# First attention: score tiles of 32 queries of four heads, over 288 key columns

## The chip, the cores and the metric

The kernel runs on one core of a Trainium2 chip. The core has four compute engines with queues of their own: TensorE (PE, matrix products into the PSUM banks; PEld is its weight load), VectorE (DVE), ScalarE (ACT) and GpSimd (POOL). SyncE (SP) computes nothing and issues most of the transfers. Sixteen DMA engines move data between the chip's DRAM and the on-chip SBUF. The metric is the device time of one execution in microseconds, lower is better.

## The reference

One layer of an encoder, batch 1, 2048 tokens, width 1024, all in float32. The input is normalised, one product with `w_in` gives the queries, keys and values of two attentions and two gates, each attention's result is projected and gated, the two are added, go through `w_out` and onto the input, and a two-layer MLP (1024 to 4096 to 1024, squared ReLU) and a last normalisation follow.

The change lies in the first attention. It has 8 query heads of width 64 and 2 key/value heads, four query heads to each. A token sees the tokens at a distance of at most 128; a slope per head times the distance is taken from the score, and a learned sink logit per head takes part in the softmax:

```
q_pos = i * A_BLOCK + jnp.arange(A_BLOCK)
k_pos = (i - 1) * A_BLOCK + jnp.arange(3 * A_BLOCK)
dist = jnp.abs(q_pos[:, None] - k_pos[None, :])
valid = (dist <= A_WINDOW) & (k_pos[None, :] >= 0) & (k_pos[None, :] < s)
sc = jnp.einsum('bqkgd,bskd->bkgqs', qi, ki).astype(jnp.float32) * scale
sc = sc - slopes[:, :, None, None] * dist.astype(jnp.float32)
sc = jnp.where(valid, sc, -jnp.inf)
...
p = jax.nn.softmax(jnp.concatenate([sc, sink_col], axis=-1), axis=-1)[..., :-1]
...
```

The probabilities `p` are then multiplied with the values. With blocks of 128 queries, a block touches 384 keys, though a single query sees only 257 of them.

## The kernel before, in words

Every float32 operand of a product is split in two parts, a high one rounded to a narrower format (fp32r) and the low rest. ACT makes the high part with a copy, DVE or POOL the low part with a subtraction, and a product takes two or three matmuls. All matmuls take 128 rows of weights and up to 512 columns.

The stages, in order of time:

1. Input projection (`in_quad`, 0 to about 360 us). Blocks of 512 tokens are called b; b = 0 and 1 are projected here with a scheme of seven products for eight (the products are numbered by `ORDER`, results fall due at numbers 2, 7, 4 and 3). PE's banks are emptied by DVE additions (the helper at L290) and ACT copies (L498). A result of the q and k features goes through `qk_parts` (L426): ACT writes the high part (L443 for the first attention, with the scale; L439 for the second), DVE the low part (L444, L440), both into one buffer `ze` of a ring of two, and SP stores it to DRAM (L464). A buffer may be filled again when its store has landed. On the same ACT queue stand the casts of the next weights (`zwhl`, L293), on the same DVE queue their low parts (L294) and the emptying of the banks.
2. First attention (L747 `attn_a`, about 360 to 660 us). A unit is one key/value head g and one block i of 128 queries: 32 units. For each of the four heads h, two matmuls (L764, L765) give scores of 128 queries by 384 keys (256 for the first and last block). The stored q has 64 rows of high and 64 of low parts, the keys are loaded in two arrangements, so two matmuls give all four part products. DVE adds the bias (a tile of distances times the head's slope, made by POOL at L731), takes the row's maximum together with the sink and writes to the SBUF tile `sa` (L766). ACT takes the exponential and the row sums (L773), a few operations of four columns handle the sink (L769 to L775), POOL multiplies by the reciprocal (L777). PE turns the probabilities, 128 by 128 at a time, into the bank `pt` (L784), ACT and DVE split them (L787, L788), and PE multiplies them with the values (L789, L790) into a bank `av`. ACT and DVE add its two halves into `ya` (L793, L794), which SP stores to `y_a`.
3. Between the units, `paced` puts dense filler: the projection of blocks b = 2 and 3 by plain three-matmul products (`mm`, L200 to L202). Its q results go through the same `qk_parts` into a ring of three buffers `z` and are stored at L705 (417 to 488 us).
4. Second attention (to about 1030 us, also with dense filler), gates and output projection, then the two MLP products to the end.

The order of the instructions on each engine is not written out by hand: the program order above is reordered by the framework's planner, which simulates the program with its own costs while it builds it. `issue_after` holds single instructions behind others.

In DRAM, q of the first attention is `qs_a[g][m]`, laid out `[128, 4, 8, 128]`: row of parts, head, block, query (m is the half of the tokens). A store of one result tile (128 features, so two heads, by 512 tokens) is two DMAs of 128 runs of 512 floats. The load of a unit (L757) takes 4 runs of 128 floats from each of 128 rows.

Of the kernel before, what the change touches and what calls it, by code (L numbers as in the profile page):

```python
# [8 lines left out]
F32 = mybir.dt.float32  # L9
F32R = mybir.dt.float32r  # L10
AF = mybir.ActivationFunctionType
ALU = mybir.AluOpType
# [10 lines left out]
P = 128  # L23
KC = D // P
NB = 4
BT = 512
ROWS = 32
GW = 64
NEG = -1.0e30


O_QA, O_KA, O_VA, O_QB, O_KB, O_VB, O_GA, O_GB = 0, 512, 640, 768, 1280, 1792, 2304, 3328
# [30 lines left out]
def host_constants():  # L63
    import numpy as np

    q = np.arange(128)[:, None]
    k = np.arange(384)[None, :] - 128
# [25 lines left out]
def encoder_layer(ctx, tc, x, norm_mix, w_in, b_gate, sink, rpb, w_pa, w_pb, w_out,  # L93
                  norm_mlp, w_up, w_down, norm_final, dist_a, mask_b, out):
    nc = tc.nc
    V, A, G, PE, SY = nc.vector, nc.scalar, nc.gpsimd, nc.tensor, nc.sync
# [16 lines left out]
    dp = pool("dp", space=DRAM)  # L113
# [20 lines left out]
    sink_t = cp.tile([P, AH], F32, name="sink_t")  # L134
# [13 lines left out]

    qs_a = [[dp.tile([P, 4, 8, P], F32, name=f"qs_a{g}{m}") for m in range(2)] for g in range(2)]
    ks_a = [dp.tile([2, P, S // 2], F32, name=f"ks_a{m}") for m in range(2)]
    vs_a = [dp.tile([2, P, 8, P], F32, name=f"vs_a{m}") for m in range(2)]
    qs_b = [dp.tile([2, P, 4, 4, P], F32, name=f"qs_b{t}") for t in range(4)]
# [271 lines left out]
    def qk_parts(col, b, src, t2):  # L426

        th, tl = t2[:, 0], t2[:, 1]
        if O_QB <= col < O_VB:
            if col < O_KB:  # L430

                pv = src.rearrange("p (r j c) -> p j r c", r=8, j=4)
                hv, hr, lr = (flipped(t) for t in (th, th.bitcast(F32R), tl.bitcast(F32R)))
            else:

                pv = src.rearrange("p (q r x) -> p q r x", q=2, r=4)
                hv, hr, lr = (t.rearrange("p (q x r) -> p q r x", q=2, r=4)
                              for t in (th, th.bitcast(F32R), tl.bitcast(F32R)))
            A.copy(hr, pv)  # L439
            V.tensor_tensor(out=lr, in0=pv, in1=hv, op=ALU.subtract)  # L440
        else:
            scale = 1.0 if col == O_KA else 0.125
            A.activation(th.bitcast(F32R), src, AF.Copy, scale=scale)  # L443
            last_low[0] = V.scalar_tensor_tensor(out=tl.bitcast(F32R), in0=src, scalar=scale, in1=th,  # L444
                                                 op0=ALU.mult, op1=ALU.subtract).ins
        parts = [(e, t2[e * 64 : e * 64 + 64]) for e in range(2)]
        if col < O_KA:
            dst, h = qs_a[col // 256][b // 2], col // P % 2 * 2
            dst = dst.rearrange("(z p) h i q -> p z h (i q)", z=2)
            return [(dst[:, :, h + e, b % 2 * BT : (b % 2 + 1) * BT], t) for e, t in parts]  # L450
        if O_QB <= col < O_KB:
            dst = qs_b[(col - O_QB) // P]
            return [(dst[e].rearrange("(z p) b j q -> p z b (j q)", z=2)[:, :, b], t) for e, t in parts]
        dst, o = (ks_a[b // 2], b % 2 * BT) if col == O_KA else (ks_b[(col - O_KB) // P], b * BT)
        return [(dst[e].rearrange("(z p) t -> p z t", z=2)[:, :, o : o + BT], t) for e, t in parts]
# [215 lines left out]
    ap_ = pools(s_a, "left", ("ka1", "va1", "qa", "sta", "sa", "ya", "dist", "ph", "pl", "biasa1"), "a")  # L671
    ap_.update(pools(s_a, "right", ("biasa0", "va0", "ka0"), "a"))
    hp = {}

# [46 lines left out]
            yield  # L721


    dist = T(ap_, [P, 384], F32, "dist", 1)
    SY.dma_start(dist, dist_a)
    bias_a = [None] * 2

    def make_bias_a(g):
        t = T(ap_, [P, 4, 384], F32, f"biasa{g}", 1)
        for h in range(4):  # L730
            G.tensor_scalar(t[:, h], dist, 2.0 ** -(4 * g + h + 1), 1.0, ALU.mult, ALU.mult)  # L731
        bias_a[g] = t

    done, began, shares = [], [], []

    kas = [T(ap_, [P, 2, S], F32R, f"ka{g}", 1) for g in range(2)]
    vas = [T(ap_, [P, 16, P], F32R, f"va{g}", 1) for g in range(2)]

    def load_kv(g, m, behind=None):
        k, kd = kas[g][:, :, m * (S // 2) : (m + 1) * (S // 2)], ks_a[m][g]  # L740
# [5 lines left out]

    def attn_a(g, i):  # L747
        c0, c1 = (1 if i == 0 else 0), (2 if i == 15 else 3)
        lo, hi = c0 * P, c1 * P
        n = hi - lo  # L750
        if bias_a[g] is None:

            with tc.issue_after(shares[2]):
                make_bias_a(g)
        base = (i - 1) * P
        q = T(ap_, [P, 4, P], F32R, "qa", 3)
        began.append(SY.dma_start(q.bitcast(F32), qs_a[g][i // 8][:, :, i % 8]).ins)  # L757
        ka, v = kas[g], vas[g]
        s = T(ap_, [P, 4, 384], F32, "sa", 4)
        st = T(ap_, [P, 8, 4], F32, "sta", 8)  # L760
        mx, nm, sm, es, ri = (st[:, k, :] for k in range(5))
        for h in range(4):
            ps = psum("s", 3)
            PE.matmul(ps[:, :n], q[:, h, :], ka[:, 0, base + lo : base + hi], start=True, stop=False)  # L764
            PE.matmul(ps[:, :n], q[:, h, :], ka[:, 1, base + lo : base + hi], start=False, stop=True)  # L765
            V.tensor_tensor_reduce(out=s[:, h, lo:hi], in0=ps[:, :n], in1=bias_a[g][:, h, lo:hi], scale=1.0,  # L766
                                   scalar=sink_t[:, 4 * g + h : 4 * g + h + 1], op0=ALU.add, op1=ALU.max,
                                   accum_out=mx[:, h : h + 1])
        A.activation(nm, mx, AF.Copy, scale=-1.0)  # L769
        V.tensor_tensor(out=es, in0=sink_t[:, 4 * g : 4 * g + 4], in1=mx, op=ALU.subtract)  # L770
        A.activation(es, es, AF.Exp)
        for h in range(4):
            A.activation(s[:, h, lo:hi], s[:, h, lo:hi], AF.Exp, bias=nm[:, h : h + 1], accum_out=sm[:, h : h + 1])  # L773
        V.tensor_tensor(out=sm, in0=sm, in1=es, op=ALU.add)
        V.reciprocal(ri, sm)  # L775
        for h in range(4):
            share = G.tensor_scalar(s[:, h, lo:hi], s[:, h, lo:hi], ri[:, h : h + 1], 1.0, ALU.mult, ALU.mult)  # L777
        shares.append(share.ins)
        yield
        po = psum("av", 1)  # L780
        for c in range(c0, c1):
            pt = psum("pt", 2)
            for h in range(4):
                PE.transpose(pt[:, h * P : (h + 1) * P], s[:, h, c * P : (c + 1) * P], ident)  # L784
            ph = T(ap_, [P, 512], F32R, "ph", 3)
            pl = T(ap_, [P, 512], F32R, "pl", 3)
            A.copy(ph, pt)  # L787
            V.tensor_tensor(out=pl, in0=pt, in1=ph.bitcast(F32), op=ALU.subtract)  # L788
            PE.matmul(po, v[:, i - 1 + c, :], ph, start=c == c0, stop=False)  # L789
            last = PE.matmul(po, v[:, i - 1 + c, :], pl, start=False, stop=c == c1 - 1).ins  # L790
        done.append(last)
        t = T(ap_, [64, 512], F32, "ya", 2)
        A.copy(t, po[64:128, :])  # L793
        V.tensor_tensor(out=t, in0=po[0:64, :], in1=t, op=ALU.add)  # L794
# [841 lines left out]
```

## Time and profile before

| | |
|---|---|
| median of three executions | 2621.41 us (2618.64, 2621.41, 2622.58) |
| span of the profiled execution, first to last instruction | 2620.1 us |
| mean granted TensorE clock | 0.999 |
| PE busy | 2586.9 us, 99% |
| DVE, ACT, POOL busy | 62%, 47%, 14% |
| DMA | 490.30 MB, 353982 packets, 28792 of them under 512 B |

The profile holds one execution. Engine lines give busy time; rows of groups read: line, engine, operation, output <- inputs, shape, count, then busy time and mean duration, then the idle time of the engine ahead of them and what ended it. Rows of windows read: stretch, its length, busy time of PE, PEld, DVE, ACT, POOL, then the granted clock, the share of the DMA engines' time and GB/s. Rows of waits read: who waited for whom, total, times, longest. Matmuls are pipelined: the recorded duration of one is longer than the distance to the next.

### The profile page before, as it was taken

To read this page: it belongs to the slowest core of one execution; us is meant where nothing else is said; L and a number is where in the kernel's file an instruction comes from. 1 tells how busy PE (TensorE), PEld (TensorE's weight loads), DVE (VectorE), ACT (ScalarE), POOL (GpSimd) and SP (SyncE) were. 2 spreads that over 40 slices of the span, in tenths; PEclk is the share of its full clock that TensorE was granted. 3 is DMA by queue.
4 is the path that set the end of the run, shared out by engine and by line. 5 is a ranking of instruction groups with operands and counts; after the bars stand their busy time and mean duration, and the time that the engine had idled before them with its cause. 6 is when DMAs were issued, how large, how long until landed. Compare 5 with 4: busy or idle time off the path is not lost.

```text
span 2620.1 us, 34509 instructions
## 1 busy us (share of the span) xinstructions
PE 2586.9 (99%) x12140; PEld 2149.8 (82%) x12140; DVE 1625.1 (62%) x2653; ACT 1239.8 (47%) x2261; POOL 358.1 (14%) x431
## 2 busy tenths in 40 slices
PE   8999999999999999999999999999999999999999
PEld 6888788778888888888888888888888888888887
DVE  8765666665544444755567777776656534555766
ACT  5335256666555555633334554644544322322454
POOL 1000114344555541000001000100000000000010
PEclk9999999999999999999999999999999999999999
DMA  5657485455876655954556655854428825445555
GB/s 184 200 156 200 141 243 159 114 155 145 240 219 180 191 144 164 318 177 151 179 178 208 245 205 202 302 191 149 153 101 300 300 101 182 146 146 171 183 194 170
DMA packets 353982, 490.30 MB, mean 187 GB/s; under 512 B 28792, under 2 KB 188664, under 8 KB 351632
## 3 DMA queue, kind: packets, MB, share of 16 engines
q1 hardware_dynamic: 346752, 471.04, 56.8%
q10 hardware_dynamic: 7056, 17.04, 1.8%
q8 instruction: 96, 1.57, 0.2%
q14 instruction: 78, 0.64, 0.1%
HBM read 328.54 MB, written 159.45 MB: 186 GB/s over the span
## 4 chain that ended last, share of the span: by engine, by line
PE 88%; DVE 4%; DMA 4%; ACT 2%; issue 1%; SPq 1%; POOL 0%; DVEq 0%; POOLq 0%; ACTq 0%
PE b L297 15%; PE b L299 15%; PE b L298 15%; PE mm L200 6%; PE mm L202 6%; PE mm L201 6%; PE zb L297 3%; PE zb L299 3%; PE zb L298 2%; PE pt L200 2%; PE pt L201 2%; PE pt L202 2%; PE av L967 2%; PE pt L955 2%; PE s L927 2%
## 5 line engine op out<-in xcount | busy, mean ns | idle before, releaser
L298 PE MATMUL b<-dwh,dah 128*128 128x512 f32 x896 | 348.5, 389 | 0.0
L299 PE MATMUL b<-dwh,dah 128*128 128x512 f32 x896 | 347.6, 389 | 0.0
L297 PE MATMUL b<-dwh,dah 128*128 128x512 f32 x896 | 339.6, 389 | 0.0
L293 ACT CAST dah<-da 128x1024 fp32r<-128x1024 f32 (+1 forms) x128 | 120.9, 945 | 368.6 <-PE b L299 241.8
L294 DVE TENSOR_TENSOR dah<-da,dah 128x1024 fp32r<-128x1024 f32 (+1 forms) x128 | 139.7, 1091 | 224.1 <-ACT dah L293 221.1
L297 PE MATMUL b<-ubh,uwhlb 128*128 128x512 f32 x592 | 230.3, 389 | 0.0
L298 PE MATMUL b<-ubh,uwhlb 128*128 128x512 f32 x592 | 230.3, 389 | 0.0
L299 PE MATMUL b<-ubh,uwhlb 128*128 128x512 f32 x592 | 229.3, 389 | 0.1
L200 PE MATMUL mm<-hT,whl 128*128 128x512 f32 x544 | 218.2, 401 | 0.0
L202 PE MATMUL mm<-hT,whl 128*128 128x512 f32 x544 | 215.1, 395 | 0.0
L201 PE MATMUL mm<-hT,whl 128*128 128x512 f32 x544 | 213.7, 393 | 0.0
L298 PEld LDWEIGHTS b<-dwh,dah 128*128 128x128 f32 x896 | 168.2, 188 | 35.0
L299 PEld LDWEIGHTS b<-dwh,dah 128*128 128x128 f32 x896 | 168.2, 188 | 34.9
L297 PEld LDWEIGHTS b<-dwh,dah 128*128 128x128 f32 x896 | 168.2, 188 | 34.9
L297 PE MATMUL zb<-zh,zwhl 128*128 128x512 f32 x476 | 186.7, 394 | 7.9 <-DVE zc L290 3.4
L298 PE MATMUL zb<-zh,zwhl 128*128 128x512 f32 x476 | 186.4, 392 | 0.0
L299 PE MATMUL zb<-zh,zwhl 128*128 128x512 f32 x476 | 183.7, 392 | 0.3 <-DVE zwhl L294 0.3
L290 DVE TENSOR_TENSOR uc<-b,uc 128x512 f32<-128x512 f32 x160 | 109.2, 689 | 104.2 <-PE b L299 103.2
L1506 POOL TENSOR_TENSOR st<-st,power 128x1 f32<-128x1 f32 x16 | 13.3, 841 | 925.0 <-DVE st L1505 924.9
L297 PEld LDWEIGHTS b<-ubh,uwhlb 128*128 128x128 f32 x592 | 111.1, 188 | 23.8 <-issue 0.4
L299 PEld LDWEIGHTS b<-ubh,uwhlb 128*128 128x128 f32 x592 | 111.1, 188 | 23.5 <-DVE uwhlb L294 0.5
L298 PEld LDWEIGHTS b<-ubh,uwhlb 128*128 128x128 f32 x592 | 111.1, 188 | 23.1
(253 smaller groups left out, 5912.5 us busy)
## 6 DMA issues: line engine op xcount, KB each, us to landing
at<-uc SPq DMA_DIRECT2D x224, 256.0 KB, 2.0
da<-at SPq DMA_DIRECT2D x96, 512.0 KB, 3.7
dw<-in_w_down_dram SPq DMA_DIRECT2D x160, 256.0 KB, 4.8
uraw<-in_w_up_dram SPq DMA_DIRECT2D x32, 1024.0 KB, 6.8
raw<-in_w_in_dram SPq DMA_DIRECT2D x34, 512.0 KB, 4.7
zraw<-in_w_in_dram SPq DMA_DIRECT2D x16, 1024.0 KB, 7.7
z<-zg SPq DMA_DIRECT2D x64, 256.0 KB, 5.1
qa<-qs_a SPq DMA_DIRECT2D x32, 256.0 KB, 8.3
```

The source lines that it names most:

```text
L200: PE.matmul(ps, lh, rh, start=first, stop=False)
L201: PE.matmul(ps, lh, rl, start=False, stop=False)
L202: PE.matmul(ps, ll, rh, start=False, stop=last)
L290: return eng.tensor_tensor(out=out, in0=a, in1=b, op=op).ins
L293: A.copy(hi, src)
L294: return eng.tensor_tensor(out=lo, in0=src, in1=hi.bitcast(F32), op=ALU.subtract).ins
L297: PE.matmul(ps, lh, rh, start=first, stop=False, skip_group_check=True)
L298: PE.matmul(ps, lh, rl, start=False, stop=False, skip_group_check=True)
L299: PE.matmul(ps, ll, rh, start=False, stop=last, skip_group_check=True)
L927: PE.matmul(ps[:, :n], q[:, i, :], kv[:, z, B_R0[i] // 4 : (B_R0[i] + B_NR[i]) // 4, 4 * B_C0[j] : 4 * (B_C0[j] + w)], start=z == 0, stop= ...
L955: PE.transpose(pt[:kp, at + (i - i0) * P : at + (i - i0 + 1) * P], s[i][:, rr : rr + kp], ident)
L967: last = PE.matmul(po[:, i0 * P : (i0 + ni) * P], v[:kp, c, :], src[:kp, o : o + ni * P], start=first, stop=(c == 7 and z == 1), skip_grou ...
```

## The change

A score tile still has 128 rows, but they are 32 consecutive queries of all four heads of the group, instead of 128 queries of one head. The 32 queries see 288 keys, so a tile is 288 columns wide instead of 384; a unit again has four tiles, u = 0 to 3, each 32 keys further on. What follows from it:

- The bias is one tile of 288 columns for each group, the distance times a slope that now differs by row; slopes and sinks are laid out by row (`by_head`, POOL).
- The probabilities of tile u stand in columns 32u to 32u + 288 of 384. The transposes take all 384, so the columns outside must be zero: the four `sa` buffers are allocated once, POOL clears those columns once (24 memsets), and the units take the buffers in turn.
- The sink's part is one ACT exponential with a bias by row, instead of a DVE subtraction and an ACT exponential.
- The columns of `av` are ordered by tile, head and query; the last copy and addition read it by head.
- q is laid out in DRAM as `[128, 32, 4, 32]`: row, group of 32 queries, head, query. A load takes one run of 512 floats from each row. A store writes runs of 32 floats, and is four DMAs of 1024 runs instead of two of 128.

```
-    qs_a = [[dp.tile([P, 4, 8, P], F32, name=f"qs_a{g}{m}") for m in range(2)] for g in range(2)]
+    qs_a = [[dp.tile([P, 32, 4, A_Q], F32, name=f"qs_a{g}{m}") for m in range(2)] for g in range(2)]
...
-            dst = dst.rearrange("(z p) h i q -> p z h (i q)", z=2)
-            return [(dst[:, :, h + e, b % 2 * BT : (b % 2 + 1) * BT], t) for e, t in parts]
+            n = BT // A_Q
+            dst = dst.rearrange("(z p) u h q -> p z u h q", z=2)[:, :, b % 2 * n : (b % 2 + 1) * n]
+            return [(dst[:, z, :, h + e], t[:, z].rearrange("p (u q) -> p u q", u=n)) for e, t in parts for z in range(2)]
...
-    dist = T(ap_, [P, 384], F32, "dist", 1)
+    dist = T(ap_, [P, A_K], F32, "dist", 1)
...
+    by_head = T(ap_, [P, 4], F32, "byhead", 1)
+    slope, sink_p = by_head[:, 0:2], by_head[:, 2:4]
+    for h in range(4):
+        at = slice(h * A_Q, (h + 1) * A_Q)
+        for g in range(2):
+            G.memset(slope[at, g : g + 1], 2.0 ** -(4 * g + h + 1))
+        G.tensor_copy(out=sink_p[at], in_=sink_t[at].rearrange("p (g h) -> p g h", g=2)[:, :, h])
...
-        t = T(ap_, [P, 4, 384], F32, f"biasa{g}", 1)
-        for h in range(4):
-            G.tensor_scalar(t[:, h], dist, 2.0 ** -(4 * g + h + 1), 1.0, ALU.mult, ALU.mult)
+        t = T(ap_, [P, A_K], F32, f"biasa{g}", 1)
+        G.tensor_scalar(t, dist, slope[:, g : g + 1], 1.0, ALU.mult, ALU.mult)
...
+    sas = [T(ap_, [P, 4, 384], F32, "sa", 4) for _ in range(4)]
+    for t in sas:
+        for u in range(4):
+            for lo, hi in ((0, u * A_Q), (u * A_Q + A_K, 384)):
+                if lo < hi:
+                    G.memset(t[:, u, lo:hi], 0.0)
...
-        q = T(ap_, [P, 4, P], F32R, "qa", 3)
-        began.append(SY.dma_start(q.bitcast(F32), qs_a[g][i // 8][:, :, i % 8]).ins)
+        q = T(ap_, [P, 4, 4, A_Q], F32R, "qa", 3)
+        s = sas[len(began) % 4]
+        began.append(SY.dma_start(q.bitcast(F32), qs_a[g][i // 8][:, i % 8 * 4 : i % 8 * 4 + 4]).ins)
...
-        for h in range(4):
+        span = [(max(u * A_Q, c0 * P), min(u * A_Q + A_K, c1 * P)) for u in range(4)]
+        for u, (lo, hi) in enumerate(span):
+            n = hi - lo
             ps = psum("s", 3)
-            PE.matmul(ps[:, :n], q[:, h, :], ka[:, 0, base + lo : base + hi], start=True, stop=False)
-            PE.matmul(ps[:, :n], q[:, h, :], ka[:, 1, base + lo : base + hi], start=False, stop=True)
+            for z in range(2):
+                PE.matmul(ps[:, :n], q[:, u].rearrange("p h q -> p (h q)"), ka[:, z, base + lo : base + hi],
+                          start=z == 0, stop=z == 1)
...
-        V.tensor_tensor(out=es, in0=sink_t[:, 4 * g : 4 * g + 4], in1=mx, op=ALU.subtract)
-        A.activation(es, es, AF.Exp)
+        A.activation(es, mx, AF.Exp, bias=sink_g, scale=-1.0)
...
-        A.copy(t, po[64:128, :])
-        V.tensor_tensor(out=t, in0=po[0:64, :], in1=t, op=ALU.add)
+        t4 = t.rearrange("d (h u q) -> d h u q", h=4, u=4)
+        by_u = po.rearrange("p (u h q) -> p h u q", u=4, h=4)
+        A.copy(t4, by_u[64:128])
+        V.tensor_tensor(out=t4, in0=by_u[0:64], in1=t4, op=ALU.add)
```

The DVE bias addition, the exponential and the normalisation go over the same 288 columns in the same way.

More of the change, by code (lines that the diff above doesn't have):

```diff
@@ L29 @@
 NEG = -1.0e30
+A_Q = 32
+A_K = A_Q + 256
 O_QA, O_KA, O_VA, O_QB, O_KB, O_VB, O_GA, O_GB = 0, 512, 640, 768, 1280, 1792, 2304, 3328
@@ L64, in host_constants @@
     import numpy as np
-    q = np.arange(128)[:, None]
-    k = np.arange(384)[None, :] - 128
+    q = np.arange(128)[:, None] % A_Q
+    k = np.arange(A_K)[None, :] - 128
     dist = np.abs(q - k)
@@ L670, in encoder_layer @@
     s_a = ExitStack()
-    ap_ = pools(s_a, "left", ("ka1", "va1", "qa", "sta", "sa", "ya", "dist", "ph", "pl", "biasa1"), "a")
+    ap_ = pools(s_a, "left", ("ka1", "va1", "qa", "sta", "sa", "ya", "dist", "ph", "pl", "biasa1", "byhead"), "a")
     ap_.update(pools(s_a, "right", ("biasa0", "va0", "ka0"), "a"))
@@ L748, in attn_a @@
         c0, c1 = (1 if i == 0 else 0), (2 if i == 15 else 3)
-        lo, hi = c0 * P, c1 * P
-        n = hi - lo
         if bias_a[g] is None:
@@ L755, in attn_a @@
         base = (i - 1) * P
-        q = T(ap_, [P, 4, P], F32R, "qa", 3)
-        began.append(SY.dma_start(q.bitcast(F32), qs_a[g][i // 8][:, :, i % 8]).ins)
+        q = T(ap_, [P, 4, 4, A_Q], F32R, "qa", 3)
+        s = sas[len(began) % 4]
+        began.append(SY.dma_start(q.bitcast(F32), qs_a[g][i // 8][:, i % 8 * 4 : i % 8 * 4 + 4]).ins)
         ka, v = kas[g], vas[g]
-        s = T(ap_, [P, 4, 384], F32, "sa", 4)
         st = T(ap_, [P, 8, 4], F32, "sta", 8)
         mx, nm, sm, es, ri = (st[:, k, :] for k in range(5))
-        for h in range(4):
+        sink_g = sink_p[:, g : g + 1]
@@ L763, in attn_a @@
+        span = [(max(u * A_Q, c0 * P), min(u * A_Q + A_K, c1 * P)) for u in range(4)]
+        for u, (lo, hi) in enumerate(span):
+            n = hi - lo
             ps = psum("s", 3)
[L764 to L768, printed above, removed]
+            for z in range(2):
+                PE.matmul(ps[:, :n], q[:, u].rearrange("p h q -> p (h q)"), ka[:, z, base + lo : base + hi],
+                          start=z == 0, stop=z == 1)
+            V.tensor_tensor_reduce(out=s[:, u, lo:hi], in0=ps[:, :n], in1=bias_a[g][:, lo - u * A_Q : hi - u * A_Q],
+                                   scale=1.0, scalar=sink_g, op0=ALU.add, op1=ALU.max, accum_out=mx[:, u : u + 1])
@@ L769, in attn_a @@
         A.activation(nm, mx, AF.Copy, scale=-1.0)
-        V.tensor_tensor(out=es, in0=sink_t[:, 4 * g : 4 * g + 4], in1=mx, op=ALU.subtract)
-        A.activation(es, es, AF.Exp)
-        for h in range(4):
-            A.activation(s[:, h, lo:hi], s[:, h, lo:hi], AF.Exp, bias=nm[:, h : h + 1], accum_out=sm[:, h : h + 1])
+        A.activation(es, mx, AF.Exp, bias=sink_g, scale=-1.0)
+        for u, (lo, hi) in enumerate(span):
+            A.activation(s[:, u, lo:hi], s[:, u, lo:hi], AF.Exp, bias=nm[:, u : u + 1], accum_out=sm[:, u : u + 1])
@@ L774, in attn_a @@
         V.tensor_tensor(out=sm, in0=sm, in1=es, op=ALU.add)
         V.reciprocal(ri, sm)
-        for h in range(4):
-            share = G.tensor_scalar(s[:, h, lo:hi], s[:, h, lo:hi], ri[:, h : h + 1], 1.0, ALU.mult, ALU.mult)
+        for u, (lo, hi) in enumerate(span):
+            share = G.tensor_scalar(s[:, u, lo:hi], s[:, u, lo:hi], ri[:, u : u + 1], 1.0, ALU.mult, ALU.mult)
         shares.append(share.ins)
@@ L782, in attn_a @@
             pt = psum("pt", 2)
-            for h in range(4):
-                PE.transpose(pt[:, h * P : (h + 1) * P], s[:, h, c * P : (c + 1) * P], ident)
+            for u in range(4):
+                PE.transpose(pt[:, u * P : (u + 1) * P], s[:, u, c * P : (c + 1) * P], ident)
             ph = T(ap_, [P, 512], F32R, "ph", 3)
```

## The prediction

> **What bounds the kernel now.** I read the page's first line and its busy shares first, then the chain that ended last, then the first attention's stretch alone: its windows and its groups by shape.
>
> ```profile
> span 2620.1 us, 34509 instructions
> PE 2586.9 (99%) x12140; PEld 2149.8 (82%) x12140; DVE 1625.1 (62%) x2653; ACT 1239.8 (47%) x2261; POOL 358.1 (14%) x431
> ...
> PE 88%; DVE 4%; DMA 4%; ACT 2%; issue 1%; SPq 1%; POOL 0%; DVEq 0%; POOLq 0%; ACTq 0%
> ```
>
> ```profile
> sum 300.00, PE 293.99 PEld 241.89 DVE 190.00 ACT 191.54 POOL 122.12; mean PE 58.80 PEld 48.38 DVE 38.00 ACT 38.31 POOL 24.42
> ```
>
> PE is busy for 99% of the span and 88% of the chain is PE. The second fence is the windows from 360 to 660 us, which is the first attention with its dense filler: PE 294 of 300 us, DVE and ACT about 64%, POOL 41%. So in this stage only PE's own work counts, and whatever makes PE wait. A busy PE is not a PE at its rate, so the length of a matmul is read from the distance between starts. The timeline of PE, start and then duration in us:
>
> ```profile
> 470.06 0.33 PE L765 MATMUL s<-ka,qa 128*128 128x384 f32 x1
> 470.23 0.33 PE L764 MATMUL s<-ka,qa 128*128 128x384 f32 x1
> 470.41 0.33 PE L765 MATMUL s<-ka,qa 128*128 128x384 f32 x1
> 470.58 0.33 PE L764 MATMUL s<-ka,qa 128*128 128x384 f32 x1
> ```
>
> ```profile
> 361.33 0.27 PE L764 MATMUL s<-ka,qa 128*128 128x256 f32 x1
> 361.44 0.28 PE L765 MATMUL s<-ka,qa 128*128 128x256 f32 x1
> 361.56 0.28 PE L764 MATMUL s<-ka,qa 128*128 128x256 f32 x1
> 361.68 0.28 PE L765 MATMUL s<-ka,qa 128*128 128x256 f32 x1
> ```
>
> A 384-column score matmul starts 0.173 us after the last one (0.52 over three), a 256-column one 0.117 us (0.35 over three). That is 0.44 ns a column. The weight load in front of each is recorded at 188 ns (below), and the 0.117 shows that it does not hold back the matmuls: they go on shrinking with the columns.
>
> ```profile
> L764 PEld LDWEIGHTS s<-ka,qa 128*128 128x128 f32 x128 | 24.1, 188 | 9.5 <-DVE sta L766 7.9 <-DVE zc L290 0.3
> L764 PE MATMUL s<-ka,qa 128*128 128x384 f32 x112 | 41.5, 370 | 1.4 <-DVE sta L766 1.3
> L784 PE MATMUL pt<-ident,sa 128*128 128x128 f32 x368 | 55.1, 272 | 0.4 <-DVE pl L788 0.4
> L789 PE MATMUL av<-ph,va 128*128 128x512 f32 x92 | 38.7, 420 | 2.0 <-DVE ya L794 1.1 <-ACT ph L787 0.8
> L790 PE MATMUL av<-pl,va 128*128 128x512 f32 x92 | 38.6, 419 | 1.6 <-DVE pl L788 1.4
> L766 DVE CUSTOM_DVE_ANT_0 sa<-s,biasa,sink_t 128x384 f32<-128x384 f32 x112 | 64.7, 612 | 25.0 <-PE pt L784 14.9 <-PE s L765 8.2 <-POOL sa L777 1.5
> L770 DVE TENSOR_TENSOR sta<-sink_t,sta 128x4 f32<-128x4 f32 x32 | 11.6, 363 | 0.2
> ```
>
> **The change part by part.** *Score matmuls, on the path.* Their number stays (32 units, four tiles, two products). 112 pairs, so 224 matmuls, go from 384 to 288 columns: 0.173 - 96 x 0.00044 = 0.131 us each, 224 x 0.042 = **-9.4 us**. The 16 pairs of the first and last block go from 256 columns to 160, 192, 224 and 256, a mean of 208: 32 x 48 x 0.00044 = **-0.7 us**. Transposes and value products (L784, L789, L790) keep number and shape: 0.
>
> *DVE, ACT, POOL.* The score evictions, exponentials and normalisations lose a quarter of their columns, and one small DVE operation a unit (L770) goes. All three engines lie beside PE here. They can give back only PE's idle time, 1.4 + 0.4 + 2.0 + 1.6 = 5.4 us in the groups above, whose releasers are mostly these operations. Between 0 and -5.4; most of those waits are for the value part, which does not change, so I take **-1**. The final copies read PSUM in 32-element runs over the same 512 elements: 0, DVE's shares above cover it.
>
> *POOL's new small work.* 24 memsets of zeros and 12 small operations for the per-head scalars, against eight bias operations that become two.
>
> ```profile
> L136 POOL MEMSET power<- 128x1 f32 x1 | 0.1, 98 | 0.0
> L731 POOL TENSOR_SCALAR biasa<-dist 128x384 f32<-128x384 f32 x8 | 4.0, 511 | 68.4 <-PE zb L298 68.2
> 370.86 1.84 POOL L777 TENSOR_SCALAR sa<-sa,sta 128x256 f32<-128x256 f32 x4 [7.73 <-ACT z L443]
> ```
>
> At 0.1 to 0.3 us each (98 ns is a memset of one column, 511 ns an operation of 384) the 36 take 4 to 11 us, against the 7.7 us that POOL idles ahead of its first normalisation; 3 us of bias work go. The 12 scalar operations, 1 to 4 us, stand ahead of the first bias and so of the first score evictions, but dense products are there for PE meanwhile: 0, at worst +4.
>
> *Loading q.* Runs of 2 KB for 512 B; the second attention's same-sized load already has that form and lands sooner. Nothing waits for it now: 0.
>
> ```profile
> qa<-qs_a SPq DMA_DIRECT2D x32, 256.0 KB, 8.3
> qb<-qs_b SPq DMA_DIRECT2D x32, 256.0 KB, 4.0
> qs_a<-ze SPq DMA_DIRECT2D x16, 256.0 KB, 5.3
> ```
>
> *Storing q, the price.* A result tile of 128 features went out in two DMAs of 128 runs of 2 KB. Now it is four DMAs of 1024 runs of 128 B: 4096 packets for 256. No row shows a 128 B store. The nearest, by the DMA view of three windows (22 to 23.7 us, nearly all 4 B; 943 to 947 us, nearly all 512 B; 39 to 46 us, the q stores themselves at 2 KB):
>
> ```profile
> DMA packets 1868, 0.12 MB, mean 72 GB/s; under 512 B 1812, under 2 KB 1812, under 8 KB 1868
> ...
> q1 hardware_dynamic: 1868, 0.12, 77.9%
> ```
>
> ```profile
> DMA packets 966, 0.49 MB, mean 123 GB/s; under 512 B 5, under 2 KB 966, under 8 KB 966
> ...
> q1 hardware_dynamic: 966, 0.49, 42.6%
> ```
>
> ```profile
> q1 hardware_dynamic: 576, 1.05, 54.0%
> ```
>
> Share x window x 16 engines over packets: 0.779 x 1.7 x 16 / 1868 = 11.3 ns; 0.426 x 4 x 16 / 966 = 28.2 ns; 0.54 x 7 x 16 / 512 = 118 ns. A tile costs each engine 16 x 118 = 1.9 us now, and 256 packets at 11.3 to 28.2 ns, 2.9 to 7.2 us, after. A straight line between the two rows gives 15.4 ns at 128 B, so 3.9 us: **2.0 us more a tile**, between 1.0 and 5.3. SP issues two more DMAs a tile at about 0.6 us (two took 1.25 us, next fence); they run while the first two move, so I count them in this.
>
> *Where it lies on a path.* Half of the stores (417 to 488 us) leave from three buffers, between 5 us dense products, and no wait there names them: 0, up to 28 ns a packet. The other half is in the input projection, where all q and k results share two buffers (ze):
>
> ```profile
> 83.41 1.25 SPq L464 DMA_DIRECT2D qs_a<-ze  x2
> ```
>
> ```profile
> ACT ze L443 <- DMA qs_a<-ze: 10.8, 4, 4.8
> ACT ze L439 <- DMA qs_b<-ze: 5.7, 3, 2.2
> ACT ze L439 <- DMA qs_a<-ze: 5.5, 1, 5.5
> ```
>
> ```profile
> 114.47 0.62 ACT L439 CAST ze<-zc 128x512 fp32r<-128x512 f32 x1 [5.50 <-DMA qs_a<-ze]
> 115.00 1.05 ACT L293 CAST zwhl<-zraw 128x1024 fp32r<-128x1024 f32 x1
> ```
>
> ```profile
> 115.13 0.69 DVE L440 TENSOR_TENSOR ze<-zc,ze 128x512 fp32r<-128x512 f32 x1 [3.27 <-ACT ze L439]
> 115.74 0.69 DVE L290 TENSOR_TENSOR zc<-zb,zc 128x512 f32<-128x512 f32 x1
> ```
>
> ```profile
> 100.00:110.00 10.00, 10.00 (x46) 8.29 (x45) 7.18 (x9) 3.27 (x4) 0.00 (x0) 1.00 0.85 230
> 129.90 0.50 PE L297 MATMUL zb<-zh,zwhl 128*128 128x512 f32 x1 [0.30 <-DVE zc L290]
> ```
>
> From 88 to 115 us each refill of a buffer waits for the store of the fill two before, so a slower store is handed on: three rounds (88, 96, 104, 114 us). Queued behind the waiting ACT are the next weights' cast (115.00), behind the waiting DVE the evictions of PE's banks (115.74). At 129.90 PE already loses 0.3 us to such an eviction, so the slack is nearly used up. If the order on ACT and DVE stays as it is, three rounds x 2.0 us = 6 us reach PE (3.0 at 11.3 ns, 15.9 at 28.2 ns). But that order is written by a planner that sees the longer stores and can put casts and evictions ahead of the waits; then nothing reaches PE. Between 0 and +15.9 I take half of the middle, **+3**, since both orders are open.
>
> Sum: -9.4 - 0.7 - 1 + 3 = -8.1 us against the profiled span of 2620.1 us, which is 1.3 us under the median of the runs, 2621.41. The same step from the median is **2613 us**.
>
> The row says that a small packet costs less time than a large one, down to 11.3 ns. The Trainium skill, DMA: Bandwidth & Descriptors, Specifications, gives 512 B as the smallest transfer at line rate and says that below it the engine reads, modifies and writes. No run here has such a store, so the trace cannot say; by it the stall would be the 37.5 us of the third rival.
>
> **The rivals.** *The wait stays static.* ACT and DVE keep their order and 15.4 ns holds: -11.1 + 6 = -5.1 us, 2616 us, on the edge of what can be told. For it: four of the waits for q stores exist already. Against: the planner's freedom. Chance 0.15.
>
> *Slower: the stores become the bound of the projection.* One mechanism, at the two ze buffers. At 28.2 ns a packet the three rounds give +15.9, so 2621.4 - 11.1 + 15.9 = 2626 us. It decides from 11.1 us of stall, 3.7 us a tile, 22 ns a packet; by 0.2% it is slower from 16.3 us. For it: DMA is 0.85 busy from 100 to 110 us, so added DMA time cannot hide there. Against: the 11.3 ns row. Chance 0.22.
>
> *A store under 512 B costs a read and a write.* At 2 x 28.2 = 56 ns a packet, a tile takes 14.4 us, 12.5 more; three rounds are 37.5 us, and 2621.4 - 11.1 + 37.5 = 2648 us. No wait in the trace speaks for it. Chance 0.08. It is the rule that the Trainium skill states in DMA: Bandwidth & Descriptors, Specifications.
>
> *The columns bring nothing*, since the 188 ns weight load sets the pace: then only the +3 is left, 2624 us. The 0.117 us starts speak against it; chance 0.02.
>
> **How the numbers follow.** The forecast has 0.53; its own range, stall from 0 to 5 us and idle from 0 to -5.4, is 2606 to 2616. The rivals hold 0.15, 0.22, 0.08 and 0.02. The range 2605 to 2628 leaves out the read-and-write case and a part of the second rival, where more than three rounds are late. A difference of 0.2%, 5.2 us, is about what a measurement of this kernel can tell from none. Faster, under 2616.2, is all of the forecast and a third of the static case: 0.58. Slower, over 2626.6, takes a stall over 16.3 us: the read-and-write case and two thirds of the second rival, 0.22. Within: 0.20.
>
> **What would show it.** Right: score matmuls 0.131 us apart with 288 columns; PE's idle groups in 360 to 660 us not larger; that stage some 10 us shorter. The stores: packets under 512 B up by 65,536 on the page (16 tiles of 4096), their landing at 5.3 us now 7 to 8; ACT's wait for them in 80 to 130 us up by 5 to 10 us, while PE's idle time on the projection's products grows by about 3 us. Wrong: PE idle or a lower granted clock between 90 and 140 us by over 10 us, a landing over 12 us, or starts of the narrower matmuls still 0.17 us apart.

## The result and the profile after

The changed kernel took 2615.27 us (median of 8, 2613.16 to 2617.02) against 2621.97 us (median of 8) for the kernel before beside it: a ratio of 0.9976, 95% interval 0.9966 to 0.9986. A second comparison, e7 below, gave 0.9980 (0.9971 to 0.9989). So it is faster by 0.2%, some 6 us. The forecast was 2613 us. The total came out; two of the terms that make it up did not, and the experiments are mostly about that.

The page of the changed kernel:

```profile
span 2613.4 us, 34714 instructions
PE 2575.6 (99%) x12140; PEld 2147.1 (82%) x12140; DVE 1604.9 (61%) x2621; ACT 1230.9 (47%) x2261; POOL 348.2 (13%) x461
DMA packets 403647, 490.26 MB, mean 188 GB/s; under 512 B 94840, under 2 KB 238328, under 8 KB 401296
```

PE is still busy 99% of the span. Packets under 512 B went from 28792 to 94840. Two stretches moved, in opposite directions. By the starts of PE's matmuls, the projection's last product ended at 361.1 us before and at 367.3 us after (+6.2, of which 1.7 us are one more stretch at half clock, see the last section); from the first score matmul to the last value product of the first attention it was 300.4 us (361.0 to 661.4) and is 287.6 us (367.1 to 654.7), so -12.8; from there to the last product of the MLP nothing changed (1952.5 and 1952.4 us).

First the attention: the groups by shape of the changed kernel from 360 to 660 us, then two places of PE's timeline there (start, duration of the whole row, and how many matmuls it holds):

```profile
L786 DVE CUSTOM_DVE_ANT_0 sa<-s,biasa,byhead 128x288 f32<-128x288 f32 x112 | 53.8, 512 | 33.4 <-PE pt L802 18.9 <-PE s L784 13.2 <-POOL sa L795 1.2
L802 PE MATMUL pt<-ident,sa 128*128 128x128 f32 x368 | 54.8, 272 | 2.0 <-DVE pl L806 2.0
L784 PE MATMUL s<-ka,qa 128*128 128x288 f32 x224 | 46.3, 311 | 1.8 <-DVE sta L786 1.4
```

```profile
448.43 0.42 PE L784 MATMUL s<-ka,qa 128*128 128x288 f32 x2
448.69 0.39 PE L204 MATMUL mm<-hT,whl 128*128 128x512 f32 x1
```

Two matmuls of 288 columns take 0.26 us from start to start (448.43 to 448.69), 0.13 each; 0.131 was forecast. An eviction (L786) takes 512 ns in place of 612.

Now the projection. ACT's waits from 80 to 140 us, the windows from 80 to 140 us of before and then of after, and PE's waits from 60 to 300 us, all but the second fence of the changed kernel:

```profile
ACT ze L446 <- DMA qs_a<-ze: 14.6, 4, 4.4
ACT ze L442 <- DMA qs_a<-ze: 9.0, 2, 6.7
ACT ze L442 <- DMA qs_b<-ze: 8.0, 5, 2.9
```

```profile
80.00:140.00 60.00, 59.70 (x267) 49.12 (x266) 44.45 (x55) 22.39 (x30) 0.00 (x0) 1.00 0.67 198
```

```profile
80.00:140.00 60.00, 57.23 (x247) 46.58 (x246) 41.85 (x53) 20.31 (x28) 0.00 (x0) 0.97 0.83 189
```

```profile
PE zb L300 <- DVE zc L293: 5.5, 2, 2.9
PE zb L302 <- DVE zwhl L297: 1.6, 2, 1.4
PE zb L300 <- ACT zc L502: 0.7, 1, 0.7
```

ACT waits 31.6 us for the stores of q (both attentions) where it waited 22.0 (+9.6; the rows of before stand in the prediction), the DMA engines are busy 0.83 of the stretch for 0.67, and PE loses 2.5 us more in these 60 us. The granted clock of the stretch fell too, from 1.00 to 0.97; that was no term of the forecast and has a section at the end.

The price of a packet is read from the DMA view of 39 to 47 us, where nearly all are 128 B:

```profile
DMA packets 8154, 1.04 MB, mean 129 GB/s; under 512 B 8153, under 2 KB 8153, under 8 KB 8153
...
q1 hardware_dynamic: 8153, 1.03, 85.9%
```

0.859 x 8 us x 16 / 8153 = 13.5 ns; a tile of 4096 packets takes each engine 3.5 us in place of 1.9.

### The profile page after: what moved, and what is told of

It reads as the page before. It is cut to its first block, busy times and chain, and to the rows that moved or that the text cites. A ratio compares the mean times of both kernels' runs of the same rounds, so it can differ in the third digit from the quotient of the medians.

```text
span 2613.4 us, 34714 instructions
## 1 busy us (share of the span) xinstructions
PE 2575.6 (99%) x12140; PEld 2147.1 (82%) x12140; DVE 1604.9 (61%) x2621; ACT 1230.9 (47%) x2261; POOL 348.2 (13%) x461
## 4 chain that ended last, share of the span: by engine, by line
PE 87%; DVE 5%; DMA 3%; ACT 2%; issue 1%; SPq 1%; POOL 0%; DVEq 0%; POOLq 0%; ACTq 0%
PE b L300 15%; PE b L302 15%; PE b L301 15%; PE mm L205 6%; PE mm L203 6%; PE mm L204 6%; PE pt L203 2%; PE pt L204 2%; PE pt L205 2%; PE zb L302 2%; PE av L987 2%; PE zb L300 2%; PE zb L301 2%; PE pt L975 2%; PE s L947 2%; PE pt L802 1%
```

## The experiments

The kernels of each part were compared on one chip with the kernel before: e1 to e4 beside 2622.25 us, e5 to e8 beside 2622.18 us, e9 and e10 beside 2622.56 us. The ratio is an estimate of its own, with its interval, and not the quotient of the two medians.

```
                                          median us   ratio to before (95%)
e1  stores in 2 KB runs, order by load     2611.53    0.9957 (0.9945 to 0.9970)
e2  stores in 2 KB runs, order by POOL     2615.43    0.9974 (0.9965 to 0.9984)
e3  before + 128 B stores                  2627.67    1.0022 (1.0014 to 1.0031)
e4  before + four DMAs a store             2622.93    1.0002 (0.9993 to 1.0011)
e5  changed, score matmuls 384 wide        2620.85    0.9997 (0.9989 to 1.0006)
e6  before + 256 B stores                  2623.03    1.0004 (0.9995 to 1.0013)
e7  changed kernel again                   2616.76    0.9980 (0.9971 to 0.9989)
e8  e1 again, beside e7                    2610.28    0.9952 (0.9939 to 0.9966)
e9  before, fewer score columns on PE      2625.43    1.0007 (0.9997 to 1.0016)
e10 before, 288 columns on DVE, ACT, POOL  2616.21    0.9972 (0.9961 to 0.9984)
```

**The stores: e3, e4, e6.** e3 is the kernel before with the new stores alone:

```
-    qs_a = [[dp.tile([P, 4, 8, P], F32, ...
+    qs_a = [[dp.tile([P, 32, 4, 32], F32, ...
...
-            return [(dst[:, :, h + e, b % 2 * BT : (b % 2 + 1) * BT], t) for e, t in parts]
+            return [(dst[:, z, :, h + e], t[:, z].rearrange("p (u q) -> p u q", u=n)) for e, t in parts for z in range(2)]
```

> The kernel before with the new stores alone: four DMAs of 1024 runs of 128 B a tile into the new layout, loaded in one run of 2 KB from each row; score tiles as before. The queries then stand in the wrong order in each tile, which changes no shape and no instruction of the attention. Theory: the projection ends about 6 us later, the attention stays at 300 us, 2626 to 2628 us. Rival A (order or layout of the rest of the change): no change, 2622 us.

Its windows and ACT's waits from 80 to 140 us:

```profile
80.00:140.00 60.00, 55.84 (x241) 45.49 (x240) 40.71 (x52) 19.63 (x27) 0.00 (x0) 0.97 0.82 186
```

```profile
ACT ze L443 <- DMA qs_a<-ze: 15.0, 4, 4.9
ACT ze L439 <- DMA qs_a<-ze: 8.7, 2, 6.3
```

The waits of the changed kernel are there without anything of its attention, and the run costs 5.4 us, as the theory had it. From 80 to 140 us PE loses 3.9 us more than in the kernel before.

e4 keeps the 2 KB runs and cuts each store into four DMAs:

```
-            return [(dst[:, :, h + e, b % 2 * BT : (b % 2 + 1) * BT], t) for e, t in parts]
+            return [(dst[:, z, h + e, b % 2 * BT : (b % 2 + 1) * BT], t[:, z]) for e, t in parts for z in range(2)]
```

> The kernel before with each tile's two q stores cut into four, still of 2 KB runs (64 each). Theory (it is the time of the packets on the DMA engines: 4096 x 13.5 ns against 256 x 118 ns): no change, 2620 to 2623 us. Rival C (it is SP's issuing, two more issues of 0.6 us a tile that the landing waits for): the projection ends 3 to 6 us later, 2625 us or more.

No difference can be measured (+0.7 us, at most +2.9 by the interval): the issuing of more DMAs is not it. That leaves the packets, and e6 tests them: it is e3 with runs of 64 floats instead of 32.

> The kernel before, with its q results stored in runs of 256 B (2048 packets a tile in place of 256 of 2 KB) by four DMAs; its scores still read 128 columns as one head's, so that queries and heads are in another order than the reference's. With 128 B the same edit cost 5.4 us over the kernel before. Theory A, the time of the packets: a straight line between 13.5 ns at 128 B and 28.2 ns at 512 B gives 18.4 ns at 256 B, 2048 x 18.4 / 16 = 2.4 us a tile where 128 B took 3.5 and 2 KB 1.9; with a third of the added time a third of the cost, 1 to 3 us over the kernel before. Theory B, any run under 512 B costs a fixed toll on the write: about as much as 128 B, 4.5 us or more. Theory C, the added 1.7 us of half clock in the 128 B kernel was most of it and comes or goes by chance: then the time differs from the kernel before by 0 or by 1.7 us, as the clock shows.

Its DMA view of 39 to 47 us and its window from 80 to 140 us:

```profile
DMA packets 3756, 0.94 MB, mean 117 GB/s; under 512 B 3755, under 2 KB 3755, under 8 KB 3755
...
q1 hardware_dynamic: 3755, 0.93, 62.1%
```

```profile
80.00:140.00 60.00, 60.00 (x268) 49.64 (x267) 44.49 (x56) 23.37 (x31) 0.00 (x0) 1.00 0.79 202
```

0.621 x 8 us x 16 / 3755 = 21.2 ns a packet, so 2048 of them are 2.7 us a tile. PE loses nothing in the stretch (60.00 of 60) and the time can't be told from that of before (+0.9 us, between -1.3 and +3.4 by the interval). A toll of 4.5 us or more on every store under 512 B (theory B of the expectation) falls. Theory A's 1 to 3 us stay possible by the run times, but the profile shows none of them: the projection ends 1.8 us later, and 1.7 us of that are one more stretch at half clock. Theory C falls as well, since half clock makes 1.6 of e3's 5.4 us (last section). So 1.9 and 2.7 us a tile are hidden, 3.5 us are not, and the slack of the two `ze` buffers ends in between.

**Without the small stores: e1, e2, e8.** e1 keeps the whole change of the attention, stores q as before and lets the loads make the order, four DMAs of 512 runs of 128 B for each unit:

```
-        began.append(SY.dma_start(q.bitcast(F32), qs_a[g][i // 8][:, i % 8 * 4 : i % 8 * 4 + 4]).ins)
+        qd = qs_a[g][i // 8][:, :, i % 8].rearrange("p h (u q) -> p u h q", u=4)
+        for u in range(4):
+            ld = SY.dma_start(q[:, u].bitcast(F32), qd[:, u]).ins
+        began.append(ld)
```

> The changed kernel, but q is stored as before (two DMAs of 128 runs of 2 KB a tile) and put into the order of 32 queries of four heads by the load: four DMAs of 512 runs of 128 B a unit. Theory (the 128 B stores hold the two ze buffers of the input projection, worth 4 to 6 us): the projection ends within 1 us of the kernel before (361 us in its profile, 367 after), the attention keeps its gain, about 2609 us. Rival A (the planner's new order or the new SBUF layout cost the projection its 6 us, whatever the stores are): the projection ends at 366 to 368 again, about 2615 us. Rival B (128 B runs cost wherever they are): the loads hold up the attention, 2615 us or more.

> The changed kernel with the q results stored as before in 2 KB runs and the order of queries made by the loads, beside the changed kernel itself. Theory A, the 128 B stores cost the changed kernel 4 us or more: 2611.5 us again, 4 us under the changed kernel. Theory B, the difference between two calls was the chip's: both within 1.5 us of each other.

2611.53 us, and 2610.28 us beside the changed kernel's 2616.76 us: 6.5 us less than the changed kernel, 11.9 us less than the one before, and the best of all. So e8's theory A holds. The end of the projection came back less fully than e1's theory had it: 365.2 us in e1 and 363.6 in e8, where 361.1 was before, and 1.7 us of each difference are one more half-clock stretch. The same number of 128 B packets (32 units of 4 x 512) costs less as loads in the attention than as stores in the projection. Three waits of e8's score matmuls (one in e1, 1.0 us) are for these loads, in the view of all its waits:

```profile
PE s L786 <- DMA qa<-qs_a: 2.4, 3, 1.9
```

That is the price that the waits show, 2.4 us where the stores cost 5 to 6. The window of e8 from 80 to 140 us is nearly that of before:

```profile
80.00:140.00 60.00, 59.63 (x265) 49.04 (x264) 44.63 (x55) 22.65 (x30) 0.00 (x0) 1.00 0.67 199
```

e2 loads q in the old order too and lets POOL copy it into the new one.

```
+        qh = T(ap_, [P, 4, P], F32, "qh", 2)
+        began.append(SY.dma_start(qh, qs_a[g][i // 8][:, :, i % 8]).ins)
+        G.tensor_copy(out=q, in_=qh.rearrange("p h (u q) -> p u h q", u=4))
```

> The changed kernel, but q is stored and loaded as before (runs of 2 KB and of 512 B), and POOL puts each unit's q into the order of 32 queries of four heads with one copy of 128 x 512 (about 0.7 us, 32 of them, 22 us of POOL's 150 us of idle time in the stage). Theory: as with the runs at the load, about 2609 us, with the projection's end back at 361 us; no packet under 512 B is added. Rival A (order or layout): 2615 us. If POOL's copy gets into the chain of the units, the attention's stretch grows from 287.6 us towards 300 us and the time towards 2620 us.

2615.43 us, as much as the changed kernel: what the stores gave back was lost again. The first score matmul started at 377.3 us, where it was 367.1 us in the changed kernel and 365.1 us in e1, though the projection itself ended at 363.7 us. How much of the 3.9 us to e1 is the extra step on POOL is not shown: PE did filler in the meantime, and the mean clock of e2's executions was 0.9972 for e1's 0.9980, which is 2 us.

**The attention's gain, taken apart: e5, e9, e10.** e5 is the changed kernel with its score matmuls over all 384 columns again, everything else as changed:

```
-                PE.matmul(ps[:, :n], q[:, u].rearrange("p h q -> p (h q)"), ka[:, z, base + lo : base + hi],
+                PE.matmul(ps[:, : (c1 - c0) * P], q[:, u].rearrange("p h q -> p (h q)"), ka[:, z, base + c0 * P : base + c1 * P],
```

> The changed kernel, in which the score matmuls alone go back to all key columns of their blocks (384, and 256 in the first and last block), while VectorE, ScalarE and GpSimd keep 288 columns a tile. Theory A, the gain is TensorE's own columns: 224 matmuls x 96 columns x 0.44 ns is 9.5 us, and 0.7 us at the edges, so about 10 us (8.5 to 12) more than the changed kernel, near 2625 us, over the kernel before by what the stores cost; score matmuls start 0.173 us apart again. Theory B, most of the first attention's 12.8 us came from the other engines' fewer columns, which no longer hold TensorE: then this kernel keeps most of the gain and stays under 2620 us, with its attention stretch under 293 us.

> The changed kernel once more, beside the others of this call: 2615.3 us, 0.9976 of the kernel before. If the half-clock stretches come by chance, their number (three in its first profile) differs; if they belong to its schedule, there are three again, near 116, 273 and 673 us.

2620.85 against 2616.76 us: the columns are worth 4.1 us there, between 1 and 8 us by the two intervals. That speaks against the 10 us of theory A, and theory B's bounds were just missed too (under 2620 us; a stretch under 293 us, where it is 294.6 us without half-clock time). So it asked for the two halves of the attention's change by themselves, each in the kernel before. e9 cuts TensorE's columns only:

```
-            PE.matmul(ps[:, :n], q[:, h, :], ka[:, 1, base + lo : base + hi], start=False, stop=True)
+            m = 192 if n == 384 else n
+            PE.matmul(ps[:, :m], q[:, h, :], ka[:, 1, base + lo : base + lo + m], start=False, stop=True)
```

> The kernel before, unchanged but for TensorE's score columns: in every pair of 384 columns the second product covers only 192 of them, so a pair has 576 columns, as many as two of 288; for the other 192 keys the scores lack the second product's part. Stores, loads and the other engines' columns are those of before. Theory A, the gain is TensorE's columns at 0.44 ns each: 112 x 192 x 0.44 ns, 9.5 us less, near 2612.5 us. Theory B, that the changed kernel's gain by columns is only some 4 to 5 us, as between the changed kernel and the one with wide score matmuls (2616.8 and 2620.9 us), because the matmuls that are shorter wait longer for their evictions: near 2617.5 us, with fewer microseconds between starts of score matmuls but more at the products around them.

e10 cuts the columns of the evictions, exponentials and normalisations only:

```
+        cut = [(max(h * 32, lo), min(h * 32 + 288, hi)) for h in range(4)]
...
-            V.tensor_tensor_reduce(out=s[:, h, lo:hi], in0=ps[:, :n], in1=bias_a[g][:, h, lo:hi], scale=1.0,
+            V.tensor_tensor_reduce(out=s[:, h, l1:h1], in0=ps[:, l1 - lo : h1 - lo], in1=bias_a[g][:, h, l1:h1], scale=1.0,
```

> The kernel before with its score evictions, exponentials and normalisations over 288 of the 384 columns (fewer in the first and last block), the rest of each tile zeros that were written once; 96 keys of each tile are left out of the result. TensorE's columns, stores and loads are those of before. Theory A, as forecast, that the other engines' fewer columns give TensorE about 1 us of idle time back (0 to 5.4): 2617 to 2622 us. Theory B, that they gave some 5 to 6 us of the change's gain (what is left of it when the stores' cost and the columns are taken out): 2615 to 2617.5 us, with the score matmuls of unchanged width some 4 us less from start to start over the stage.

The columns alone bring nothing: 2625.43 us, a ratio of 1.0007 (0.9997 to 1.0016), which neither theory of e9 had. A mean clock of 0.9979 for 0.9988 makes 2.4 us of the 2.9 between the medians; without that the time is that of before. The other engines' columns alone bring 6.3 us, 2616.21 us, as theory B of e10 had it. PE's waits of e9 from 360 to 660 us (the profile is of its slowest execution, so half-clock time is taken out of the sums below):

```profile
PE s L765 <- DVE sta L767: 5.1, 7, 1.1
PE pt L785 <- DVE pl L789: 3.2, 2, 1.8
PE av L791 <- DVE pl L789: 1.9, 3, 1.0
PE av L790 <- DVE ya L795: 1.4, 3, 0.6
PE av L790 <- ACT ph L788: 0.6, 1, 0.6
```

And the same view of the kernel before:

```profile
PE s L764 <- DVE sta L766: 1.9, 3, 1.1
PE av L790 <- DVE pl L788: 1.4, 3, 0.8
PE av L789 <- DVE ya L794: 1.1, 4, 0.6
PE av L789 <- ACT ph L787: 0.8, 2, 0.5
PE pt L784 <- DVE pl L788: 0.4, 1, 0.4
```

12.2 us in place of 5.6. One place of e9's timeline shows how it comes (start, duration, engine, line; of the rows between 475.5 and 477.5 us those of the score matmuls and DVE's long operations):

```profile
475.50 0.42 PE L765 MATMUL s<-ka,qa 128*128 128x384 f32 x1
475.61 0.61 DVE L767 CUSTOM_DVE_ANT_0 sa<-s,biasa,sink_t 128x384 f32<-128x384 f32 x1
475.76 0.25 PE L766 MATMUL s<-ka,qa 128*128 128x192 f32 x1
475.85 0.36 PE L765 MATMUL s<-ka,qa 128*128 128x384 f32 x1
476.05 0.25 PE L766 MATMUL s<-ka,qa 128*128 128x192 f32 x1
476.15 0.69 DVE L444 SCALAR_TENSOR_TENSOR z<-mm,z 128x512 fp32r<-128x512 f32 x1
476.40 0.34 PE L765 MATMUL s<-ka,qa 128*128 128x384 f32 x1
476.58 0.25 PE L766 MATMUL s<-ka,qa 128*128 128x192 f32 x1
476.75 0.61 DVE L767 CUSTOM_DVE_ANT_0 sa<-s,biasa,sink_t 128x384 f32<-128x384 f32 x1
477.43 0.45 PE L765 MATMUL s<-ka,qa 128*128 128x384 f32 x1 [0.60 <-DVE sta L767]
```

A pair of products is done in about 0.3 us here, an eviction takes 0.61 us, and DVE has a filler result of 0.69 us between two of them. There are three score banks. PE runs ahead of DVE, comes to the end of the banks and waits 0.60 us for the eviction of 476.75. A quicker matmul only reaches that wait earlier. In the sums of the distances between PE's starts, with half-clock time taken out, e9's score matmuls have 4.4 us less than those of before, and its transposes 3.7 us more; the stretch of the attention is 299.8 us, before 300.4.

The groups of evictions and score matmuls in e10, and PE's waits of the same stretch:

```profile
L775 DVE CUSTOM_DVE_ANT_0 sa<-s,biasa,sink_t 128x288 f32<-128x288 f32 x112 | 53.9, 513 | 31.1 <-PE pt L793 17.8 <-PE s L773 12.7
L772 PE MATMUL s<-ka,qa 128*128 128x384 f32 x112 | 40.8, 365 | 0.9 <-DVE sta L775 0.8
L773 PE MATMUL s<-ka,qa 128*128 128x384 f32 x112 | 37.8, 337 | 0.0
```

```profile
PE pt L793 <- DVE pl L797: 1.9, 1, 1.9
PE s L772 <- DVE sta L775: 0.8, 2, 0.4
PE av L799 <- DVE pl L797: 0.7, 2, 0.4
```

112 evictions of 513 ns for 612 are 11.1 us less of DVE, which was only 63% busy in this stretch. The score matmuls have the width of before, and their starts lie 48.7 us apart in sum where it was 55.2 us, 6.5 us less; 44 of the 256 distances are over 0.25 us, where it was 68. What a score matmul needs of another engine while a unit runs is a bank that DVE has emptied, so the shorter eviction is the likely cause. That is argued: e10 shortens ACT's exponentials and POOL's normalisations as well, and no row shows these short waits one by one.

In a sum of measured parts: other engines -6.3 (e10), columns with those in place -4.1 (e5 to e7), stores +5.4 (e3), together -5.0 us. Measured were -5.4 us beside e7 and -6.7 us in the first comparison. The parts that can be added otherwise agree: e5 should be -6.3 + 5.4 = -0.9 us and was -1.3. By the stretch of the attention, half-clock time taken out, it is 300.4 us before, 299.8 in e9, 292.4 in e10, 294.6 in e5 and 287.6 in the changed kernel. Seven filler products, 1.6 us, lie outside the stretch in the last three. So the columns alone are worth 0.6 us there, the other engines alone 6.4, and the columns after them 7.0.

What stays open: the order of the instructions is written anew by the planner for each of these kernels, so e9 and e10 differ from before in more than their own lines. When PE's products of the stretch are compared as lists, e9's agrees with that of before in 93% of its places, e10's in 60%, and e10's with that of the changed kernel in 89%. How much of the 6.3 us is the shorter eviction, how much the shorter work of ACT and POOL, and how much the new order, was not separated.

## Why the prediction was right, and where it was not

- *Score matmuls, -9.4 and -0.7.* The rate was right: 0.13 us between starts, 0.131 forecast. That all of it lies on the path was wrong: the columns are worth nothing alone (e9) and 4.1 us once the other engines' work is shorter (e5 to e7; between 1 and 8). The failed step is "only PE's own work counts, and whatever makes PE wait", read from a PE that is busy 294 of 300 us and a DVE at 63%. Where e9's timeline shows it, with three banks, the pace within a unit's four tiles was DVE's.
- *DVE, ACT, POOL, -1 and at most -5.4.* This is the mis-sized term: -6.3 (e10, interval -4.2 to -10.2 by its ratio). The bound was taken from PE's idle time in the groups, and that step failed. A score matmul recorded at 0.34 us starts 0.17 us after the one before, so a wait of up to that difference leaves no idle time in the view. In e10 PE's waits in the stretch fell by 2.2 us only (5.6 to 3.4), the distances between the starts by 6.5 us.
- *POOL's small work, 0.* Nothing of PE waits for it; of DVE's first evictions, 1.2 us wait for the bias. Right so far as waits show it.
- *Loading q, 0.* In e3, which loads q in the same runs, they land in 7.6 us (median of the five of 32 that have a landing) where it was 8.3; the changed kernel's trace has no landing of them. No wait of the changed kernel names them. Right.
- *Storing q, the price.* 13.5 ns a packet for the 15.4 estimated, 3.5 us a tile for 3.9. Right, and the straight line between two far rows, both of loads, was good enough. A store's landing is 6.4 us in e3 (the five of 32 that have one; the changed kernel's trace has none), short of the 7 to 8 forecast; each DMA holds 128 KB where it was 256.
- *Storing q, on the path, +3 between 0 and +15.9.* It costs 5.4 us (e3; 6.5 us between e7 and e8). From 80 to 130 us ACT's waits for these stores grew from 16.3 to 23.6 us, so 7.3, as forecast (5 to 10); PE's waits in the projection from 3.4 to 7.8 us, so 4.4, where about 3 was forecast. In size that is what the static rival had (+6), and the term was half of it because a planner that hides the stores was given the other half. The order was not static, though: before, two fills of `ze` on ACT follow each other at 96.3 and 97.5 us; in the changed kernel a cast of weights stands between them. The new order did not hide the stores. e6 has the same new order and no cost.
- *The rivals.* A store that costs a read and a write, 56 ns a packet: 13.5 ns. The Trainium skill (DMA: Bandwidth & Descriptors, Specifications) says that transfers under 512 B are read, modified and written; these went to DRAM at 13.5 and 21.2 ns a packet, so the price that the rival put on it was not paid. "The columns bring nothing" had 0.02, by the weight load. Its cause was wrong: the product behind a 192-column one of e9 starts 0.088 us later (median), half of the 0.175 us behind a 384-column one of before, though each has a weight load in front of it. The outcome was right for the columns by themselves.

So it is luck that 2613 came near 2615 to 2617 us: by the run times the columns were 6 us too good, the relief 5 us too small and the stores 2.4 us too small, and these errors cancel in part. By the stretch of the attention the columns were 3 us too good.

## What to carry to other kernels

When one step feeds another through a few buffers, cut both or look which of the two sets the pace: a PE that the profile shows busy at 98% can hold waits that are shorter than a matmul's recorded length, so read the distances between starts, and do not take the idle column for a bound on what a faster partner gives back. A new layout has to be paid for on one side, and it is worth trying both: the same small runs cost 5 to 6 us as stores out of two buffers, where the DMA engines were 0.83 busy, and 1.0 to 2.4 us of waits as loads into three buffers, where they were 0.69 to 0.70 busy. Which of the two, buffers or DMA load, made the difference was not tested. A slack is a threshold: 2.7 us a tile were free, 3.5 were not.

## What was unexpected of the hardware

A wait of PE can be followed by a stretch at half clock, and so cost more than itself. In the changed kernel's first profile PE waits 2.62 us in the projection; about a microsecond after it restarts, its matmuls lie 0.43 us apart instead of 0.23, for 3.4 us:

```profile
115.26 0.47 PE L300 MATMUL zb<-zh,zwhl 128*128 128x512 f32 x1 [2.62 <-DVE zc L293]
...
117.06 0.63 PE L300 MATMUL zb<-zh,zwhl 128*128 128x512 f32 x1
117.49 0.63 PE L301 MATMUL zb<-zh,zwhl 128*128 128x512 f32 x1
```

The window of 110 to 120 us shows the granted clock, 0.83 for 10 us, so 1.7 us lost. In e7, the same kernel, the same wait was longer and the clock stayed full (PE's timeline, and the window):

```profile
115.36 0.47 PE L300 MATMUL zb<-zh,zwhl 128*128 128x512 f32 x1 [3.23 <-DVE zc L293]
...
116.59 0.40 PE L302 MATMUL zb<-zh,zwhl 128*128 128x512 f32 x1
116.82 0.39 PE L300 MATMUL zb<-zh,zwhl 128*128 128x512 f32 x1
```

```profile
110.00:120.00 10.00, 6.77 (x30) 5.29 (x29) 5.62 (x9) 2.20 (x3) 0.00 (x0) 1.00 0.95 194
```

```profile
110.00:120.00 10.00, 7.38 (x26) 5.64 (x25) 5.42 (x9) 2.19 (x3) 0.00 (x0) 0.83 0.98 206
```

The second window is that of the first profile. The profile of before has one such half-clock stretch ahead of its last microseconds, that of the changed kernel three, e7 one, and at another place. In the profile of before a wait of 1.58 us at 52.6 us has such a stretch 1.8 us behind it, and one of 2.92 us at 267.6 us has none. So waits of 1.6 to 3.2 us are sometimes followed by one, at 1.7 us each, and no run shows what decides it. The eleven executions of e7 spread from 2611 to 2621 us, and their granted clocks go with it: 2612.3 us at 0.999, 2615.3 at 0.998, 2617.2 at 0.997 and 2620.5 at 0.996 (medians of 2, 3, 4 and 2). Over all executions the mean clock is 0.9988 for the kernel before and 0.9975 for the changed one, 0.0013 x 2615 = 3.4 us that the change loses by the clock, beside what its waits cost; e3 loses about 1.6 us so (0.9982), e10 about 1.8 (0.9981). The Trainium skill (TensorE: Matmul & The Clock Gate, Part 1) describes a gate that halves the clock after an idle window of about 3.4 us that runs freely. The length of the stretches agrees. The idle time does not: here 1.58 and 2.62 us of recorded idle time were once enough, and 2.92 and 3.23 us once not, so a whole window without work was not needed.
